# Seven half-size products in place of eight for 19 of 22 unit pairs of a feed-forward's first layer

## The chip, the cores and the metric

One core of one Trainium2 chip runs the whole program. The metric is the device time of one execution in microseconds (us), the median of several runs. The engines are TensorE (PE, matmuls, with PEld for its weight loads), VectorE (DVE), ScalarE (ACT), GpSimd (POOL, here only an issuer of DMA transfers) and SyncE (SP, the main issuer of transfers).

## What is computed

A two-layer encoder is applied to two sequences with shared weights. Each has 16 learned tokens and 256 tokens of 1024 features. A layer adds a mixer (retention and attention, gated) and then a feed-forward to h:

```python
def _swiglu(h, w_ffn_in, w_ffn_out):
    a, u = jnp.split(h @ w_ffn_in, 2, axis=-1)
    return (jax.nn.silu(a) * u) @ w_ffn_out

    for l in range(DEPTH):          # DEPTH = 2
        h = h + _mixer(_rms(h, norm_mix[l]), w_in[l], ...)
        h = h + _swiglu(_rms(h, norm_ffn[l]), w_ffn_in[l], w_ffn_out[l])
    return _rms(h, norm_final)[:, N_META:]
```

D_MODEL is 1024 and D_FF is 2816, so w_ffn_in has 2 x 2816 columns: 22 blocks of 128 for a and 22 for u. All data are 32-bit floats.

## The kernel before

**Tiles.** Activations lie with features on the 128 partitions: eight tiles of 128 features by tokens (272 in layer 0; 256 in the last layer, whose learned tokens are not needed there). Weights are cut into units, one for each block of 128 output columns: eight 128x128 tiles, 512 KB. A unit of the first feed-forward layer is called ("fa", f) for the gate half and ("fu", f) for the other half, f from 0 to 21; the output layer's are "fo0" to "fo2" for three groups of f (8, 7 and 7).

**Precision.** Each operand is split into a high part, rounded to the matmul's format by a ScalarE copy, and a low part, the VectorE subtraction that is left. A product is three matmuls for each feature tile: high by high, high by low, low by high (lines 222 to 224). A unit is thus 24 matmuls for one moving block. In layer 0 the moving block is one sequence (272 columns), and every unit runs twice. In layer 1 most units run once over both sequences (512 columns); where a stage starts they run for each sequence (256 columns). `split` (line 226) makes the parts of activations, `prefetch` (lines 203 to 216) those of weights: per half unit a 256 KB transfer on SP's queue into `wst` (three buffers), `A.copy` to `wh`, and a subtraction to `wl` (four buffers each), two units ahead.

**Norm.** The feed-forward's norm scales a token by r. The kernel before multiplies h by the gain and splits it at once, in `fin_wo` at the end of each unit of the mixer's last layer ("wo"), by `u_split`; r (`norm_scale`, a matmul of ones by the summed squares, two transposes and some ten small VectorE operations) comes later, and the products are scaled after the matmul (`fin_fa`, `fin_fu`).

**Order.** The program is a list of units written out in order (`prog`); steps that belong between units are put off by a number of units (`later`, `due`). A scheduler turns that into one instruction order for each engine at build time. It may place an instruction ahead of earlier ones that it reckons are not ready. At run time each engine goes through its own list in order and waits on semaphores. PSUM has eight banks: three "lin", three "att" and two for the scores of attention ("sc").

For each f before: fa's matmuls, VectorE scales the result, ScalarE tanh, two VectorE operations, fu's matmuls, one VectorE operation and the split into the group's tiles `oh`, `ol` (or `gh`, `gl`; the groups alternate). When a group's f are done its "fo" units run, which add to h.

Of the kernel before, what the change touches and what calls it, by code (L numbers as in the profile page):

```python
# [20 lines left out]
ALU = mybir.AluOpType  # L22
# [65 lines left out]
def hybrid_kernel(tc, ctx, a, y_dram):  # L88
# [13 lines left out]
    def f32(t):  # L102
        return t.bitcast(F32)
# [97 lines left out]
    wq, wready = [], {}  # L201

    def prefetch(n):
        while len(wready) < min(n, len(wq)):
            key = wq[len(wready)]
            ap, kt = unit_ap(key)
            wh = wts.tile([P, KT, P], F32R, tag="wh", name="wh", bufs=NW)
            wl = wts.tile([P, KT, P], F32R, tag="wl", name="wl", bufs=NW)
            for k in range(0, kt, NK):
                n = min(NK, kt - k)  # L210
                st = wts.tile([P, NK, P], F32, tag="st", name="wst", bufs=NST)
                nc.sync.dma_start(st[:, :n], ap[:, k:k + n])
                A.copy(wh[:, k:k + n], st[:, :n])  # L213
                V.tensor_tensor(wl[:, k:k + n], st[:, :n], f32(wh)[:, k:k + n], ALU.subtract)  # L214
            wready[key] = (wh, wl, kt)
# [106 lines left out]
    def later(d, f, *args):  # L322
        steps.append((slot[0] + d, f, args))
# [24 lines left out]
    def layer(l):  # L348
# [376 lines left out]

        def open_group(gi):
            n = GROUPS[gi][1] - GROUPS[gi][0]
            pool, tg = ((act, "o"), (E["wk"], "g"))[gi % 2]
            E["g", gi] = grid(tg + "h", F32R, pool=pool, n=n), grid(tg + "l", F32R, pool=pool, n=n)

        def fin_fa(ps, s, f):
            st["fa", s, f] = t = scratch("fa", s, q0)
            V.tensor_tensor(t, of(ps, s, q0), scale(s, q0), ALU.mult)  # L733

        def fin_fu(pu, s, f):
            gi = next(i for i, (f0, f1) in enumerate(GROUPS) if f0 <= f < f1)
            i = f - GROUPS[gi][0]
            ta, t = st.pop(("fa", s, f)), scratch("ft", s, q0)
            tanh(t, ta)
            V.scalar_tensor_tensor(t, t, 1.0, ta, ALU.add, ALU.mult)  # L740
            V.tensor_tensor(t, t, scale(s, q0), ALU.mult)
# [199 lines left out]
    for key, f, rest in prog:  # L941
        if key is None:
            f(*rest)
        else:
# [6 lines left out]
            due(slot[0])  # L951
# [40 lines left out]
```

## Time and profile before

| | us |
|---|---|
| median of 3 runs (1847.3 to 1849.12) | 1849.12 |
| the profiled execution | 1849.4 |
| its span, first to last instruction | 1847.6 |
| TensorE busy in the span | 1830.0 |
| VectorE busy | 1141.9 |
| ScalarE busy | 796.9 |

The span is what the trace shows; the 1.8 us beside it lie before the first and after the last instruction. Busy time counts an instruction from its start to its end; matmuls are pipelined, so that the durations of neighbours overlap, and what one costs is read from the distance of the starts. The same holds in a smaller measure for VectorE.

### The profile page before, as it was taken

Reading aid. Unit: us, or ns where it says so; the run is one execution under the profiler, and the core shown is the slowest. Engines: PE = TensorE matmul, PEld = TensorE weight load, DVE = VectorE, ACT = ScalarE, POOL = GpSimd, SP = SyncE. Lnnn points to the kernel's source line nnn. Section 1 sums busy time; section 2 is a strip of 40 time slices with the busy share of each in tenths; the row PEclk is TensorE's granted clock in tenths of the full one; section 3 lists DMA queues with packets and bytes.
Section 4 is the critical chain, followed back from the end, with each engine's and each line's share of the span. In section 5 each row is a group of like instructions: output and inputs, shape, how many; then the busy total and the mean of one; then the engine's idle time right before and its main releaser. Section 6 shows DMA issues by size and latency. Waiting matters only on the chain.

```text
span 1847.6 us, 32203 instructions
## 1 busy us (share of the span) xinstructions
PE 1830.0 (99%) x12546; PEld 1701.7 (92%) x12546; DVE 1141.9 (62%) x2789; ACT 796.9 (43%) x1791; POOL 9.9 (1%) x31
## 2 busy tenths in 40 slices
PE   9999999999999999999999999999999999999997
PEld 8999999999999999999998888988888988988887
DVE  7777777776466535545577677676754654444545
ACT  7767753443343313323346566444433433222323
POOL 0000000000000000000000000000000000000000
PEclk9999999999999999999999999999999999999999
DMA  4222212224222323232233222222233232332332
GB/s 152 92 70 64 74 60 69 81 70 133 88 81 92 92 69 104 82 101 86 83 124 98 75 74 64 69 69 81 80 126 94 90 103 91 94 99 82 104 95 70
DMA packets 89624, 162.75 MB, mean 88 GB/s; under 512 B 9728, under 2 KB 18176, under 8 KB 89472
## 3 DMA queue, kind: packets, MB, share of 16 engines
q1 hardware_dynamic: 86608, 153.20, 26.6%
q0 software_dynamic: 1632, 6.42, 1.0%
q8 instruction: 98, 1.61, 0.4%
q10 hardware_dynamic: 1232, 1.08, 0.2%
q14 instruction: 54, 0.44, 0.1%
HBM read 156.47 MB, written 4.19 MB: 87 GB/s over the span
## 4 chain that ended last, share of the span: by engine, by line
PE 94%; DVE 2%; ACT 2%; DMA 1%; issue 1%; SPq 0%; DVEq 0%; ACTq 0%
PE fo L223 5%; PE fu L223 5%; PE fa L224 5%; PE fa L223 5%; PE fu L224 5%; PE fu L222 5%; PE fa L222 5%; PE fo L222 5%; PE fo L224 5%; PE rv L223 2%; PE rv L222 2%; PE rv L224 2%; PE wo L222 2%; PE wo L224 2%; PE ao L222 2%; PE ao L224 2%
## 5 line engine op out<-in xcount | busy, mean ns | idle before, releaser
L213 ACT CAST wh<-wst 128x512 fp32r<-128x512 f32 x576 | 339.9, 613 | 645.6 <-issue 182.1
L214 DVE TENSOR_TENSOR wl<-wst,wh 128x512 fp32r<-128x512 f32 x576 | 381.7, 680 | 130.2 <-ACT wh L213 115.3
L222 PE MATMUL fu<-xh,wh 128*128 128x272 f32 (+2 forms) x544 | 173.8, 319 | 0.0
L224 PE MATMUL fa<-xh,wl 128*128 128x272 f32 (+2 forms) x544 | 173.5, 319 | 0.0
L224 PE MATMUL fu<-xh,wl 128*128 128x272 f32 (+2 forms) x544 | 173.5, 319 | 0.0
L223 PE MATMUL fu<-xl,wh 128*128 128x272 f32 (+2 forms) x544 | 173.4, 319 | 0.0
L222 PE MATMUL fa<-xh,wh 128*128 128x272 f32 (+2 forms) x544 | 173.3, 319 | 0.0
L223 PE MATMUL fa<-xl,wh 128*128 128x272 f32 (+2 forms) x544 | 173.3, 319 | 0.0
L222 PE MATMUL fo<-oh,wh 128*128 128x272 f32 (+2 forms) x420 | 126.5, 301 | 0.0
L223 PE MATMUL fo<-ol,wh 128*128 128x272 f32 (+2 forms) x420 | 126.2, 301 | 0.0
L224 PE MATMUL fo<-oh,wl 128*128 128x272 f32 (+2 forms) x420 | 126.2, 300 | 0.0
L748 DVE SCALAR_TENSOR_TENSOR f<-fo,f 128x272 f32<-128x272 f32 (+2 forms) x84 | 39.6, 471 | 118.5 <-PE fo L224 118.0
L222 PEld LDWEIGHTS fu<-xh,wh 128*128 128x128 f32 x544 | 102.3, 188 | 7.2
L223 PEld LDWEIGHTS fu<-xl,wh 128*128 128x128 f32 x544 | 102.2, 188 | 7.1
L222 PEld LDWEIGHTS fa<-xh,wh 128*128 128x128 f32 x544 | 102.3, 188 | 7.0
L224 PEld LDWEIGHTS fu<-xh,wl 128*128 128x128 f32 x544 | 102.2, 188 | 7.0
L224 PEld LDWEIGHTS fa<-xh,wl 128*128 128x128 f32 x544 | 102.2, 188 | 7.0
L223 PEld LDWEIGHTS fa<-xl,wh 128*128 128x128 f32 x544 | 102.2, 188 | 6.9
L733 DVE TENSOR_TENSOR fa<-fa,rn 128x272 f32<-128x272 f32 (+2 forms) x68 | 35.0, 514 | 110.6 <-PE fa L224 110.5
L742 DVE TENSOR_TENSOR ft<-ft,fu 128x272 f32<-128x272 f32 (+2 forms) x68 | 34.6, 509 | 78.7 <-PE fu L224 78.3
L222 PEld LDWEIGHTS fo<-oh,wh 128*128 128x128 f32 x420 | 79.0, 188 | 2.8
L223 PEld LDWEIGHTS fo<-ol,wh 128*128 128x128 f32 x420 | 78.9, 188 | 2.8
(362 smaller groups left out, 5146.3 us busy)
## 6 DMA issues: line engine op xcount, KB each, us to landing
wst<-in_w_in SPq DMA_DIRECT2D x208, 256.0 KB, 2.7
wst<-in_w_ffn_in SPq DMA_DIRECT2D x176, 256.0 KB, 2.8
wst<-in_w_ffn_out SPq DMA_DIRECT2D x64, 256.0 KB, 2.7
wst<-in_w_att_o SPq DMA_DIRECT2D x32, 256.0 KB, 2.7
wst<-in_w_ret_o SPq DMA_DIRECT2D x32, 256.0 KB, 2.7
wst<-in_w_out SPq DMA_DIRECT2D x32, 256.0 KB, 2.7
wst<-in_w_ffn_out SPq DMA_DIRECT2D x32, 192.0 KB, 2.4
f<-in_x POOLq DMA_DIRECT2D x2, 1088.0 KB, 7.8
```

The source lines that it names most:

```text
L213: A.copy(wh[:, k:k + n], st[:, :n])
L214: V.tensor_tensor(wl[:, k:k + n], st[:, :n], f32(wh)[:, k:k + n], ALU.subtract)
L222: T.matmul(out, wh[:, k], at(hi, s, k, c0), start=(k == 0), stop=False)
L223: T.matmul(out, wh[:, k], at(lo, s, k, c0), start=False, stop=False)
L224: T.matmul(out, wl[:, k], at(hi, s, k, c0), start=False, stop=(k == kt - 1))
L733: V.tensor_tensor(t, of(ps, s, q0), scale(s, q0), ALU.mult)
L742: V.tensor_tensor(t, t, of(pu, s, q0), ALU.mult)
L748: V.scalar_tensor_tensor(hh, of(ps, s, q0), 0.5, hh, ALU.mult, ALU.add)
```

## The change

19 of the 22 pairs (fa, fu) of each layer are no longer computed as four block products by eight feature tiles. The pair is seen as a 2x2 block matrix (fa or fu by lower or upper half of the features) times a 2x2 block matrix (lower or upper features by sequence 0 or 1). Instead of eight half-size block products there are seven (`product`, i = 0 to 6), each of four feature tiles: 12 matmuls over one sequence's columns, in both layers. The first three pairs (NPLAIN) stay as they were.

For the weights four combinations are needed, called a, b, c and d: a is fa itself, d the upper half of fu, c = fu with fu's lower half added onto its upper half and fa's lower half onto its lower half, b from a and c. c is formed by a 512 KB load and two accumulating transfers from POOL's queue. b is formed by VectorE. All four are split. `plan` places these steps at fixed leads ahead of a pair, counted in units (a product counts a quarter).

For the activations three sums and one replaced half are needed (`mix`, with the tiles T), and for those the norm must be applied before the products: `norm_x` replaces `u_split`. The products' results are combined on the way out of PSUM. Products 5 and 6 use the two "sc" banks.

The groups of the output layer no longer alternate between two buffers, the temporary pools of the feed-forward have other sizes, and prefetching goes by position (`prefetch(pos[key])`) with the same two units of lead for plain units.

```diff
-NW, AHEAD, NTMP, NLIN = 4, 2, ((8, 0), (4, 4)), 3
+NW, AHEAD, NTMP, NTMPF, NLIN = 4, 2, ((8, 0), (4, 4)), ((4, 3), (4, 5)), 3
+NPLAIN = 3
...
+    def s_load(key):
+        _, l, f, _ = key
+        fa, fu = a["w_ffn_in"][l, f], a["w_ffn_in"][l, NF + f]
+        c, v, d = s_tmp("wc"), s_tmp("wa"), wts.tile([P, NK, P], F32, tag="st", name="wst", bufs=NST)
+        nc.sync.dma_start(c, fu)
+        nc.gpsimd.dma_start(c[:, NK:], fu[:, :NK], accum_op=ALU.add)
+        nc.gpsimd.dma_start(c[:, :NK], fa[:, :NK], accum_op=ALU.add)
+        nc.sync.dma_start(v, fa)
+        nc.sync.dma_start(d, fu[:, NK:])
+        wready[l, f] = {"c": [c], "a": [v], "d": [d]}
+    def s_tmp(name, tag="q", bufs=3):
+        return E["wk"].tile([P, KT, P], F32, tag=tag, name=name, bufs=bufs)
+    def s_hi(w, nm):
+        pool, tg, n, bufs = {"a": (wts, "w", KT, NW), "b": (wts, "w", KT, NW),
+                             "c": (E["wk"], "c", KT, 1), "d": (E["wk"], "d", NK, 1)}[nm]
+        w[nm] += [pool.tile([P, n, P], F32R, tag=tg + x, name=tg + x, bufs=bufs) for x in "hl"]
+        A.copy(w[nm][1], w[nm][0])
+    def s_lo(w, nm):
+        v, h, t = w[nm]
+        V.tensor_tensor(t, v, f32(h), ALU.subtract)
+        w[nm] = (h, t)
+    def s_1(key):
+        w = wready[key[1:3]]
+        s_hi(w, "a")
+        va, vb, vc = w["a"][0], s_tmp("wb", "wb", 1), w["c"][0]
+        w["b"] = [vb]
+        V.tensor_tensor(vb[:, :NK], va[:, :NK], vc[:, NK:], ALU.add)
+        V.scalar_tensor_tensor(vb[:, NK:], va[:, NK:], -1.0, vb[:, :NK], ALU.mult, ALU.subtract)
+    def s_2(key):
+        w = wready[key[1:3]]
+        s_hi(w, "b")
+        s_lo(w, "a")
...
+    def s_3(key):
+        w = wready[key[1:3]]
+        s_hi(w, "c")
+        s_lo(w, "b")
...
+    def s_4(key):
+        w = wready[key[1:3]]
+        s_hi(w, "d")
+        s_lo(w, "c")
+        s_lo(w, "d")
...
+                if key[3] == 0:
+                    lead = (2.5, 1, 0.75, 0.5, 0.25) if last[0] == "sp" else (3, 2, 2, 1, 1)
+                    jobs.extend((at_ - d, fn, key) for d, fn in zip(lead, (s_load, s_1, s_2, s_3, s_4)))
+                at_ += 0.25
...
         def fin_wo(ps, s, j):
...
-            u_split(s, j, DEPTH + l, q0)
             norm_add(s, hh, q0, j)
             if j == KT - 1:
                 later(LN, norm_scale, s, acc.pop(s), q0)
+                for k in range(0, KT, 2):
+                    later(LN + 1 + k // 4, norm_x, s, k)
+                if s:
+                    for i in range(3):
+                        later(LN + 4 + i, mix, i)
...
         def open_group(gi):
             n = GROUPS[gi][1] - GROUPS[gi][0]
-            pool, tg = ((act, "o"), (E["wk"], "g"))[gi % 2]
-            E["g", gi] = grid(tg + "h", F32R, pool=pool, n=n), grid(tg + "l", F32R, pool=pool, n=n)
+            E["g", gi] = grid("oh", F32R, n=n), grid("ol", F32R, n=n)
...
+        def norm_x(s, k):
+            if s and k % NK == 0:
+                E["xn", k // NK] = E["wk"].tile([P, NK, N - q0], F32, tag="q", name="xn", bufs=3)
+            for i in (k, k + 1):
+                t = E["xn", k // NK][:, i % NK] if s else tmpt("xn")[:, q0:]
+                V.scalar_tensor_tensor(t, E["h"][s][:, i, q0:], gains[:, DEPTH + l, i:i + 1],
+                                       E["r"][s][:, q0:], ALU.mult, ALU.mult)
+                if s == 0:
+                    split(E["uh"][0][:, i, q0:], E["ul"][0][:, i, q0:], t)
+            if s:
+                t = E["xn", k // NK][:, k % NK:k % NK + 2]
+                split(E["uh"][1][:, k:k + 2, q0:], E["ul"][1][:, k:k + 2, q0:], t)
+        def mix(i):
+            b12, b22 = E["xn", 0], E["xn", 1]
+            h0, l0 = f32(E["uh"][0]), f32(E["ul"][0])
+            if i == 0:
+                st["T1"] = t = E["wk"].tile([P, NK, N - q0], F32, tag="wb", name="t1", bufs=1)
+                V.tensor_tensor(t, b12, h0[:, :NK, q0:], ALU.subtract)
+                V.tensor_tensor(t, t, l0[:, :NK, q0:], ALU.subtract)
+                V.tensor_tensor(b12, b12, b22, ALU.subtract)
+                V.tensor_tensor(b22, b22, t, ALU.subtract)
+                split(*E["T"][0], b12)
+            elif i == 1:
+                split(*E["T"][1], b22)
+            elif i == 2:
+                V.tensor_tensor(b22, h0[:, NK:, q0:], b22, ALU.subtract)
+                V.tensor_tensor(b22, b22, l0[:, NK:, q0:], ALU.add)
+                split(*E["T"][2], b22)
+            else:
+                split(E["uh"][1][:, :NK, q0:], E["ul"][1][:, :NK, q0:], st.pop("T1"))
...
+        def product(f, i):
...
+            nm, half, (xh, xl) = (("a", 0, X(0, 0)), ("b", 0, E["T"][1]), ("c", 1, X(1, 0)), ("c", 0, E["T"][0]),
+                                  ("a", 1, X(0, 1)), ("b", 1, X(1, 1)), ("d", 0, E["T"][2]))[i]
+            ps = (att if i % 2 else lin)("sp")[:, :N - q0] if i < 5 else st["p34"][:, i - 5]
+            wh, wl = w[nm]
+            for k in range(NK):
+                o = half * NK + k
+                T.matmul(ps, wh[:, o], xh[:, k], start=k == 0, stop=False)
+                T.matmul(ps, wh[:, o], xl[:, k], start=False, stop=False)
+                T.matmul(ps, wl[:, o], xh[:, k], start=False, stop=k == NK - 1)
+            if i == 0:
...
+                A.copy(st["tu"][:, 0], ps)
...
+            if i == 1:
+                V.tensor_tensor(u2, ps, t1, ALU.subtract)
...
+            elif i == 3:
...
+                V.tensor_tensor(v, ps, u2, ALU.add)
+                V.tensor_tensor(y, p5, u2, ALU.add)
+                V.scalar_tensor_tensor(st["c"][:, 3], v, -1.0, p5, ALU.mult, ALU.subtract)
+            elif i == 4:
+                V.tensor_tensor(st["c"][:, 0], ps, t1, ALU.add)
...
+                tanh(st["v"][:, 0], st["c"][:, 0])
+            elif i == 6:
...
+                V.tensor_tensor(c[:, 1:3], st["p34"], st["yw"], ALU.add)
+                A.activation(v[:, 1], c[:, 1], AF.Tanh, scale=-0.5)
+                V.scalar_tensor_tensor(v, v, 1.0, c[:, :2], ALU.add, ALU.mult)
+                V.tensor_tensor(v, v, c[:, 2:], ALU.mult)
+                s_out(BOTH if q0 else 3, f, v)
...
             for f in fs[n:]:
+                for i in range(7):
+                    L(("sp", l, f, i), None, (product, f, i))
```

## Rows read from the trace of the kernel before

**Rows 1.** The page: TensorE's line of the engine table and the granted clock by slices.

```profile
PE 1830.0 (99%) x12546; PEld 1701.7 (92%) x12546; DVE 1141.9 (62%) x2789; ACT 796.9 (43%) x1791; POOL 9.9 (1%) x31
...
PEclk9999999999999999999999999999999999999999
```

**Rows 2.** The page: the chain that ended last, share of the span by engine.

```profile
PE 94%; DVE 2%; ACT 2%; DMA 1%; issue 1%; SPq 0%; DVEq 0%; ACTq 0%
```

**Rows 3.** Busy time by windows: fa and fu of group 0, each layer.

```profile
core 0: us, PE busy (x) PEld busy (x) DVE busy (x) ACT busy (x) POOL busy (x), PEclk, DMA share, GB/s
554.60:651.80 97.20, 97.20 (x773) 97.12 (x771) 57.71 (x127) 31.58 (x65) 0.00 (x0) 1.00 0.30 88
1468.60:1561.00 92.40, 92.40 (x498) 79.11 (x497) 52.24 (x99) 30.02 (x56) 0.00 (x0) 1.00 0.32 98
```

**Rows 4.** Timeline of TensorE, layer 0: start, duration; the second is 24 matmuls on.

```profile
600.41 0.29 PE L222 MATMUL fu<-xh,wh 128*128 128x272 f32 x1
...
603.45 0.29 PE L222 MATMUL fa<-xh,wh 128*128 128x272 f32 x1
```

**Rows 5.** Timeline of TensorE, layer 1, both sequences; the second is 24 matmuls on.

```profile
1502.46 0.39 PE L222 MATMUL fa<-xh,wh 128*128 128x512 f32 x1
...
1508.02 0.39 PE L222 MATMUL fu<-xh,wh 128*128 128x512 f32 x1
```

**Rows 6.** Timeline of TensorE, layer 1, one sequence; the second is 45 matmuls on.

```profile
1454.15 0.28 PE L222 MATMUL wo<-mh,wh 128*128 128x256 f32 x1
...
1459.45 0.28 PE L222 MATMUL wo<-mh,wh 128*128 128x256 f32 x1
```

**Rows 7.** Timeline of VectorE, layer 0: start, busy us; idle before, releaser.

```profile
601.18 1.29 DVE L214 TENSOR_TENSOR wl<-wst,wh 128x512 fp32r<-128x512 f32 x2
602.40 0.44 DVE L740 SCALAR_TENSOR_TENSOR ft<-ft,fa 128x272 f32<-128x272 f32 x1
...
604.83 0.44 DVE L228 TENSOR_TENSOR ol<-ft,oh 128x272 fp32r<-128x272 f32 x1
605.18 0.69 DVE L214 TENSOR_TENSOR wl<-wst,wh 128x512 fp32r<-128x512 f32 x1
...
607.65 0.44 DVE L740 SCALAR_TENSOR_TENSOR ft<-ft,fa 128x272 f32<-128x272 f32 x1 [0.56 <-ACT ft L231]
...
610.58 0.44 DVE L228 TENSOR_TENSOR ol<-ft,oh 128x272 fp32r<-128x272 f32 x1 [0.48 <-ACT oh L227]
```

**Rows 8.** Groups of VectorE instructions by form: count, busy us, mean ns, idle before.

```profile
L214 DVE TENSOR_TENSOR wl<-wst,wh 128x512 fp32r<-128x512 f32 x544 | 366.1, 687 | 128.8 <-ACT wh L213 113.9 <-PE sc L457 1.1
...
L741 DVE TENSOR_TENSOR ft<-ft,rn 128x272 f32<-128x272 f32 x44 | 19.4, 442 | 1.4
...
L315 DVE SCALAR_TENSOR_TENSOR xn<-f,cst,rn 128x272 f32<-128x272 f32 x24 | 11.3, 496 | 0.0
...
L748 DVE SCALAR_TENSOR_TENSOR f<-fo,f 128x256 f32<-128x256 f32 x24 | 10.1, 422 | 25.7 <-PE fo L224 25.5
...
L228 DVE TENSOR_TENSOR ol<-f,oh 128x544 fp32r<-128x544 f32 x8 | 5.3, 722 | 0.0
```

**Rows 9.** Groups of ScalarE instructions by form.

```profile
L213 ACT CAST wh<-wst 128x512 fp32r<-128x512 f32 x544 | 325.9, 619 | 643.3 <-issue 182.1 <-PE fo L223 116.1 <-PE fa L223 62.9
...
L231 ACT ACTIVATE ft<-fa 128x272 f32<-128x272 f32 x44 | 18.9, 429 | 41.7 <-DVE fa L733 41.7
...
L227 ACT CAST oh<-f 128x544 fp32r<-128x544 f32 x8 | 4.8, 646 | 6.5 <-DVE f L673 6.5
```

**Rows 10.** Timeline of VectorE, layer 1: last steps of the two sequences' r.

```profile
1466.56 0.43 DVE L272 STREAM_TRANSPOSE rn<-rr 128x256 f32<-128x256 f32 x1
...
1475.12 0.45 DVE L272 STREAM_TRANSPOSE rn<-rr 128x256 f32<-128x256 f32 x1
```

**Rows 11.** The page: DMA issues, KB each, median us to landing.

```profile
wst<-in_w_ffn_in SPq DMA_DIRECT2D x176, 256.0 KB, 2.8
...
f<-in_x POOLq DMA_DIRECT2D x2, 1088.0 KB, 7.8
...
f<-in_x SPq DMA_DIRECT2D x2, 544.0 KB, 6.4
```

More of the change, by code (lines that the diff above doesn't have):

```diff
@@ L199, in unit_ap @@
         return a["w_in"][l, W_IN[kind] + j], KT
[L201 to L215, printed above, removed]
+    jobs, wready = [], {}
@@ new lines, in load @@
+    def load(key):
+        ap, kt = unit_ap(key)
+        wh = wts.tile([P, KT, P], F32R, tag="wh", name="wh", bufs=NW)
+        wl = wts.tile([P, KT, P], F32R, tag="wl", name="wl", bufs=NW)
+        for k in range(0, kt, NK):
+            n = min(NK, kt - k)
+            st = wts.tile([P, NK, P], F32, tag="st", name="wst", bufs=NST)
+            nc.sync.dma_start(st[:, :n], ap[:, k:k + n])
+            A.copy(wh[:, k:k + n], st[:, :n])
+            V.tensor_tensor(wl[:, k:k + n], st[:, :n], f32(wh)[:, k:k + n], ALU.subtract)
+        wready[key] = (wh, wl, kt)
@@ new lines, in s_4, with plan @@
+    def s_4(key):
[3 more added lines that the diff above has]
+        s_lo(w, "d")
+    pos = {}
+    def plan():
+        at_, last = 0.0, None
+        for op in prog:
+            key = op[0]
+            if key is None or key in pos:
+                continue
+            pos[key] = at_
+            if key[0] != "sp":
+                jobs.append((at_ - AHEAD, load, key))
+                at_ += 1
+            else:
[3 more added lines that the diff above has]
+                at_ += 0.25
+            last = key
+        jobs.sort(key=lambda j: j[0])
@@ L731, in fin_fa, with s_out @@
+        def s_out(s, f, t):
+            gi = next(i for i, (f0, f1) in enumerate(GROUPS) if f0 <= f < f1)
+            gh, gl = E["g", gi]
+            c0 = q0 if s < 2 else 0
+            split(gh[s][:, f - GROUPS[gi][0], ..., c0:], gl[s][:, f - GROUPS[gi][0], ..., c0:], t)
         def fin_fa(ps, s, f):
             st["fa", s, f] = t = scratch("fa", s, q0)
-            V.tensor_tensor(t, of(ps, s, q0), scale(s, q0), ALU.mult)
+            tanh(t, of(ps, s, q0))
+            V.scalar_tensor_tensor(t, t, 1.0, of(ps, s, q0), ALU.add, ALU.mult)
@@ L735, in fin_fu @@
         def fin_fu(pu, s, f):
[L736 to L741, printed above, removed]
+            t = st.pop(("fa", s, f))
             V.tensor_tensor(t, t, of(pu, s, q0), ALU.mult)
-            gh, gl = E["g", gi]
-            split(at(gh, s, i, q0), at(gl, s, i, q0), t)
+            s_out(s, f, t)
@@ L897, in layer @@
         for gi, (f0, f1) in enumerate(GROUPS):
-            do(open_group, gi)
+            if gi:
+                do(open_group, gi)
             fs = list(range(f0, f1))
-            blocks = [(fs[:2], range(2))] + [([f], pair) for f in fs[2:]] if gi == 0 else [([f], pair) for f in fs]
+            n = NPLAIN if gi == 0 else 0
+            blocks = [(fs[:2], range(2))] + [([f], pair) for f in fs[2:n]] if n else []
             for b, ss in blocks:
@@ L924, in hybrid_kernel @@
     do(lambda: (E["c1"].close(), E["ct"].close()))
-    for op in prog:
-        if op[0] is not None and op[0] not in wq:
-            wq.append(op[0])
+    plan()
     ps = att("warm")
@@ L950, in hybrid_kernel @@
             post(ps, *args)
-            due(slot[0])
+        due(slot[0])
     due(1 << 30)
```

51 lines of the change are left out of this document (42 added, 9 removed).

## Prediction

> **What bounds the kernel now.** First the page's engine table and its slices, to see which engine has no slack: TensorE is busy 99% of the span at a granted clock of full speed in every slice [rows 1]. A busy share is no proof, so next the chain that ended last: 94% of it is TensorE [rows 2]. Then the windows of the two first-layer stretches that the change touches: layer 0 holds TensorE 97.20 of 97.20 us, VectorE 57.71, ScalarE 31.58, DMA share 0.30; layer 1 holds 92.40 of 92.40, VectorE 52.24 [rows 3]. So in these stretches a removed matmul is worth its pitch, and the question is what the other engines do when their load rises. A matmul's duration overlaps the next one's, so I take pitches from starts: 24 matmuls of 272 columns in 3.04 us, 0.1267 us each [rows 4]; 24 of 512 in 5.56 us, 0.2317 [rows 5]; 45 of 256 in 5.30 us, 0.1178 [rows 6].
>
> **Removed: matmuls.** A pair is fa and fu of one f. Before, layer 0 issues 2 units x 2 sequences x 24 = 96 matmuls of 272 columns, 96 x 0.1267 = 12.16 us; layer 1 issues 48 of 512 columns, 48 x 0.2317 = 11.12 us. After, both issue 7 products x 4 feature tiles x 3 = 84: layer 0 of 272 columns, 10.64 us; layer 1 of 256 columns, 9.90 us. The saving is 1.52 and 1.22 us a pair; with 19 pairs a layer 28.9 + 23.2 = 52.1 us. That is all the change can give. Layer 1 saves less because it gives up its 512-column form.
>
> The Trainium skill (TensorE: Matmul & The Clock Gate, Back-to-back issue gap) speaks against that split: it gives a sustained 81 ns per matmul at N=128 and 131 ns at N=512. By a line through these two, an estimate from that page, 84 matmuls of 256 columns would take 8.2 us and 48 of 512 columns 6.3 us, so layer 1 would lose some 36 us. Here 512 columns take 231.7 ns, 1.97 times the 256-column pitch [rows 5, 6]; the trace does not agree, and the measurement decides.
>
> **Added: VectorE, and it is nearly TensorE's load.** Per pair, VectorE forms vb (two 128x512 operations), subtracts the high parts of a, b and c (three of 1024 elements) and of d (one of 512); it unloads the products with five operations one sequence wide and four two sequences wide. By occupation (start to start) 512 elements cost 1.22/2 = 0.61 us and 272 cost 0.35 [rows 7]; that is 1.08 ns an element, so 256 cost 0.33, 544 0.64 and 1024 1.16. Weights: 3 x 0.61 + 3 x 1.16 = 5.3 us. Unloading: layer 0 5 x 0.35 + 4 x 0.64 = 4.3, layer 1 5 x 0.33 + 4 x 0.61 = 4.1. Sum 9.6 us against TensorE's 10.64 in layer 0, 9.4 against 9.90 in layer 1: 90% and 95%. The lower bound of the cost is nothing (VectorE fits under TensorE). The upper takes full durations, 0.687 for 512, 0.722 for 544, 0.442 for 272, 0.422 for 256 [rows 8], and 1.22 for 1024 by their slope: layer 0 10.9, layer 1 10.6; and adds the two places where a pair's chain crosses to ScalarE and back (tanh, then the high copy). Unfilled they idle VectorE 0.56 and 0.48 us [rows 7], with the wider copy about 1.15 together: 12.0 and 11.7 us. The same rows show the first kind filled, two weight halves at 601.18 between fa and ft, so the instruction order does put weight work into such holes. I take values near the lower end: TensorE waits 0.15 us a pair in layer 0 and 0.4 in layer 1, where only 0.5 us is spare: 2.9 + 7.6 = 10.5 us.
>
> ScalarE copies a, b, c (1024 elements) and d, and per pair has three one-sequence operations and one wide copy: by 0.619 for 512, 0.646 for 544 and 0.429 for 272 [rows 9], 3 x 1.03 + 0.62 + 3 x 0.43 + 0.65 = 5.7 us of 10. TensorE's products hide it; uncovered it would cost that.
>
> **Moved: the norm.** Before, the unnormalised u is split inside wo's units and the scale r is applied after the matmul. Now uh needs r first. r of sequence 0 is ready at 1467.0 [rows 10], 1.6 us before layer 1's stretch begins [rows 3], and then eight tiles each need a scaled multiply (0.496 us [rows 8]), a ScalarE copy and a 0.35 subtraction, some 0.85 us of VectorE a tile, beside wo's last residuals and the weights of fa and fu. TensorE eats a tile in 3 x 0.1178 = 0.35 us, or in 0.7 if fa and fu take turns. Sequence 1's r comes at 1475.6 [rows 10], some 4 us before its first unit is due four units after wo; its tiles and the mixes (about 12 us of VectorE for ten operations of 1024 or 1088 elements) stand before the first product. Queued behind them on VectorE are the plain pairs' unloadings and the first pair's weights, and for those TensorE waits. VectorE's work from wo to the first product is about 40 us (two norms 13, mixes 12, six plain units' weights 7, their unloading 5, first pair's weights 5) against some 34 to 36 us of TensorE. Nothing if reordering covers it, 10 a layer if not; I take 5, so 10 us. The removed u_split (0.5 us of VectorE per wo unit) helps a little and is not counted.
>
> **Group ends.** The last pair's chain from product 7 to the low part is 0.72 + 0.43 + 0.72 + 0.72 + 0.65 + 0.72 and four hops of about 0.1 (a tanh wait of 0.56 [rows 7] less its 0.43), 4.3 us; the output unit that follows needs that tile after 21 or 18 matmuls, 2.7 or 2.3 us in layer 0, 4.2 us with 512 columns in layer 1. Unless other units fill in, 1.6 + 2.0 + 2.0 = 5.6 us. The second pair of each group has its loads issued only when the first pair's products start; I put 0.5 us on each of six. Together 8 us (0 to 12). All groups now share one buffer, but its first new write comes a whole pair after the last read, so that costs nothing; without the cover it would be one pair, 10 us, per group.
>
> **Transfers.** A pair moves 1.75 MB in place of 1 MB: two 512 KB and one 256 KB load on SP's queue, two 256 KB accumulating transfers on POOL's queue, which first wait for c's load; POOL is otherwise idle, so nothing is behind them but the next pair's. At share 0.30 before [rows 3], 0.30 x 1.75 x 12.16/10.64 gives 0.60, with room. No row shows an accumulate. From below it costs as a plain 256 KB load, 2.8 us; from above as POOL's 1088 KB, 7.8 us [rows 11]. Load of c (between 2.8 and the 544 KB row's 6.4, say 3.6) plus one accumulate that vb needs: 6.4 to 11.4 us, and if two run one after the other at the upper price 19 to 22. The load is issued ten products (14 to 15 us) ahead and b is needed one product in, with 3.6 us of vb, copy and subtraction before: 12 to 13 us are there. I take nothing, keeping the upper end as a rival.
>
> The Trainium skill (DMA: Bandwidth & Descriptors, Anatomy of one DMA) fits 2.0 us plus bytes/436e3, which makes a 256 KB transfer 2.6 us and 1088 KB 4.6; the POOL row above says 7.8, so the page would make the accumulate cheaper than the trace suggests, and with it the term stays nothing.
>
> **Sum.** -52.1 + 10.5 + 10 + 8 = -23.6 us. The profiled execution took 1849.4 us (span 1847.6 and 1.8 around it), 0.3 above the median of 1849.12. 1849.4 - 23.6 = 1826 us.
>
> **Rivals.** (1) All cover holds: only a few us of the 28.5 are lost, 1797 to 1811. For it: VectorE's bare sum is under TensorE's in both layers, and the order already fills holes. Against: 95% use of an in-order queue. Chance 0.22. (2) VectorE becomes the bound, the one that ends on the other side: at 12.0 and 11.7 us a pair layer 0 saves 0.16 x 19 = 3 and layer 1 loses 0.6 x 19 = 11, and with the 18 us of moved work it comes to 1875. It decides from a mean of 11.17 us a pair: 19 x (12.16 + 11.12 - 2 x 11.17) = 18. For it: no slack in layer 1 and four crossings to ScalarE on each pair. Against: the holes at 601.18 are filled. Chance 0.22, a third of it mild, 1840 to 1846. (3) The accumulating transfers are late: at 22 us c and a each hold one of three slots for about 25 us, two slots a pair, 16.7 us a pair, 19 x (16.7 - 10.8 + 16.7 - 10.3) = 234 us more, 2060; at 13 to 14 us only some us. Chance 0.07. (4) In this stage a 256-column matmul costs more than half of a 512-column one, as when weight loads no longer hide: at the next wider pitch, 0.1267, layer 1's 84 take 10.64 us, 14 us less is saved, 1840. The 256-column rows speak against it. Chance 0.04. It is the mechanism of the TensorE page of the Trainium skill named above. The forecast keeps 0.45, its own range 1812 to 1840.
>
> Faster by over 0.2% (3.7 us, about what a measurement here can tell from no change): 0.45 + 0.22 + 0.07 + 0.04 = 0.78; within 0.2% 0.04; slower 0.18. The range runs from 1799, near the full saving, to 1856, into rival (2); about 0.18 lies outside.
>
> **What would show it.** Right: some 84 matmuls a pair at 0.127 and 0.118 us; pair to pair 10.6 to 11 us in layer 0 and 10 to 10.7 in layer 1; VectorE over 90% busy there; TensorE gaps of some us after wo and at group ends; granted clock still full. Wrong if VectorE is 98% busy with pairs above 11.2 us, or if vb waits for POOL's transfer, or if TensorE has no gaps at all.

## The result and the profile after

The changed kernel takes 1893.33 us (median; 1890.15 to 1896.92), the kernel before 1848.8 us beside it: ratio 1.0247, interval 1.0234 to 1.026. It is 2.5% slower, where 1826 was forecast. The profiled execution has a span of 1890.3 us against 1847.6.

The page after, in its engine table, the clock by slices, the chain by engine and the DMA issues (KB each, median us to landing):

```profile
PE 1812.6 (96%) x13002; PEld 1712.7 (91%) x13002; DVE 1293.2 (68%) x2948; ACT 862.6 (46%) x1833; POOL 76.5 (4%) x107
...
PEclk9999999999999999899999999999999999999999
...
PE 69%; DVE 12%; DMA 11%; ACT 4%; issue 4%; DVEq 0%; POOL 0%; ACTq 0%; POOLq 0%
...
wc<-in_w_ffn_in SPq DMA_DIRECT2D x38, 512.0 KB, 3.6
wc<-in_w_ffn_in POOLq DMA_DIRECT2D x76, 256.0 KB, 5.8
wa<-in_w_ffn_in SPq DMA_DIRECT2D x38, 512.0 KB, 4.6
```

TensorE is busy for only 17 us less than in [rows 1], and the span grew by 43: it now stands idle for 78 us, not 18. The chain of [rows 2] was 94% TensorE; now VectorE and DMA hold 23% of it. VectorE, the engine that I had feared for, is busy for only 68% of the span.

Cut at the first matmul of each stretch, in both traces, the first layer (ff) and the output layer (fo) of the six groups take, in us:

| | 0: ff, fo | ff, fo | ff, fo | 1: ff, fo | ff, fo | ff, fo |
|---|---|---|---|---|---|---|
| before | 97.2, 48.4 | 84.6, 42.3 | 84.6, 42.7 | 89.3, 44.4 | 77.8, 38.9 | 77.8, 39.3 |
| after | 94.8, 54.8 | 84.2, 52.2 | 82.9, 46.9 | 93.0, 53.1 | 81.6, 47.5 | 81.1, 40.1 |

Summed: the first layer 517.6 against 511.3, the output layer, whose matmuls the diff does not touch, 294.6 against 256.0. So the first layer shows nothing of the 52 us saved, and nearly the whole net loss appears where no matmul was changed. (The second window of [rows 3] runs 2.9 us into the output layer; cut here, that stretch is 89.3.) Windows after, layer 0 (group 0's ff, group 1's ff and fo, and the stretch in which TensorE restarts in that fo) and layer 1 (group 1's ff and fo):

```profile
core 0: us, PE busy (x) PEld busy (x) DVE busy (x) ACT busy (x) POOL busy (x), PEclk, DMA share, GB/s
552.80:647.60 94.80, 91.71 (x713) 89.95 (x712) 84.01 (x148) 44.45 (x74) 12.26 (x14) 1.00 0.57 151
702.40:786.60 84.20, 78.47 (x590) 77.29 (x590) 61.28 (x97) 34.64 (x54) 10.50 (x12) 0.96 0.59 139
786.60:838.80 52.20, 45.20 (x339) 44.98 (x338) 24.07 (x41) 10.93 (x18) 1.43 (x2) 0.90 0.32 94
...
792.90:803.10 10.20, 5.86 (x26) 5.86 (x27) 4.86 (x8) 1.69 (x4) 0.00 (x0) 0.50 0.27 72
...
1628.60:1710.20 81.60, 74.53 (x590) 73.01 (x590) 59.70 (x98) 33.77 (x54) 10.48 (x12) 0.96 0.59 142
1710.20:1757.70 47.50, 41.12 (x255) 36.33 (x254) 21.73 (x36) 10.71 (x18) 0.64 (x2) 0.93 0.35 106
```

The reader is to see three things. In a group of seven pairs VectorE is busy for 61.28 of 84.20 us, 73%, so it does not set the pace. DMA is at 0.59, where I had put 0.60. And the granted clock is below one: at 792.90 it is 0.50, the lower of the two levels (1.2 GHz), for 10.2 us around a stop of TensorE. That output layer is explained to the tenth: 42.3 before, 7.0 us of standing still, and half of the 5.86 busy us at half clock make 52.2. The mean clock of the whole run is 0.982, against 0.998 before: some 68 us at the lower level ((1 - 0.982) x 1890.3 / 0.5) in place of some 8.

Who waited, by engine and releaser (us in total, times, longest):

```profile
DVE wb L250 <- DMA wc<-in_w_ffn_in: 57.4, 19, 4.0
...
ACT wh L214 <- DMA wst<-in_w_ffn_out: 33.2, 18, 5.4
...
PE fo L299 <- ACT oh L304: 25.6, 5, 7.0
PE sp L867 <- DVE c L884: 19.0, 11, 3.5
...
SPq L224 <- DVE cl L242: 59.6, 11, 9.7
```

The first line is the sign that the prediction gave for its own failure: vb (tile `wb`) waits for POOL's transfer. The last is the other half: SP's load of the next c waits for VectorE, for `cl`, the low part of an earlier c. Timelines of VectorE, SP and POOL in group 1 of layer 0 (start, duration, idle before):

```profile
747.23 0.69 DVE L250 TENSOR_TENSOR wb<-wa,wc 128x512 f32<-128x512 f32 x1 [2.78 <-DMA wc<-in_w_ffn_in]
...
750.24 1.22 DVE L242 TENSOR_TENSOR cl<-wc,ch 128x1024 fp32r<-128x1024 f32 x1
...
751.49 0.33 SPq L224 DMA_DIRECT2D wc<-in_w_ffn_in  x1
...
755.53 0.88 POOL L225 DMA_DIRECT2D wc<-in_w_ffn_in  x1 [11.61 <-DVE dl L242]
...
761.41 0.69 DVE L250 TENSOR_TENSOR wb<-wa,wc 128x512 f32<-128x512 f32 x1 [3.44 <-DMA wc<-in_w_ffn_in]
762.02 0.43 DVE L883 TENSOR_TENSOR yw<-sp,tu 128x272 f32<-128x272 f32 x1
...
763.96 1.22 DVE L242 TENSOR_TENSOR cl<-wc,ch 128x1024 fp32r<-128x1024 f32 x1
...
765.20 0.33 SPq L224 DMA_DIRECT2D wc<-in_w_ffn_in  x1
```

Read it as a ring. SP issues the load of c at 751.49, at the end of a `cl`, which was the last reader of one of the three raw buffers. It lands after 3.5 us, and 4.0 us after the load POOL issues the accumulating transfer (the label there names VectorE's `dl`, which ended 0.2 us after the landing); 5.9 us later that has landed and VectorE, idle for 3.44 us, starts `wb`. Only behind that, and behind the unloadings that had piled up, comes `cl` of the pair before (2.55 us on), takes 1.22 and frees the buffer for the next load, at 765.20. One turn: 4.04 + 5.88 + 2.55 + 1.22 + 0.02 = 13.7 us a pair, against 10.6 us of matmuls. SP's loads of c in this group start at 710.87, 724.14, 738.06, 751.49, 765.20 and 779.12, 13.7 us apart in the mean. TensorE starts the group's first four pairs 10.6 us apart, because the order makes a pair's parts ahead of its products, and falls behind after that. The instruction that frees the buffer stands on VectorE behind the instruction that waits for the transfer into the next one.

At the end of the group the lag arrives at TensorE. Timelines of SP, ScalarE and TensorE there:

```profile
784.65 1.15 SPq L213 DMA_DIRECT2D wst<-in_w_ffn_out  x2
788.41 0.33 SPq L227 DMA_DIRECT2D wa<-in_w_ffn_in  x1
...
791.77 0.51 ACT L214 CAST wh<-wst 128x384 fp32r<-128x384 f32 x1 [5.35 <-DMA wst<-in_w_ffn_out]
792.18 0.42 ACT L308 ACTIVATE v<-c 128x272 f32<-128x272 f32 x1
...
796.54 0.65 ACT L304 CAST oh<-v 128x544 fp32r<-128x544 f32 x1 [1.20 <-DVE v L894]
...
797.24 0.59 PE L299 MATMUL fo<-oh,wh 128*128 128x272 f32 x1 [7.00 <-ACT oh L304]
```

ScalarE waits 5.35 us for output weights. SP holds further ones behind a load of a that waits for its buffer until 788.41, but those that ScalarE waits for were issued at 784.65, ahead of that. They were slow to land, beside the accumulating transfers that POOL issued at 783.12 and 783.66 (DMA issue at 784.65):

```profile
wst<-in_w_ffn_out SPq DMA_DIRECT2D x1, 192.0 KB, 7.1
```

Output weights issued from 783 to 796 took at most 7.1 us; in the like stretch of the kernel before (781 to 794) 2.7, and of run 4 below, which has no accumulating transfer (766 to 779), 4.4. Behind ScalarE's wait stands the last pair's tanh (792.18); the pair's high copy ends at 797.2, and TensorE had run dry 7 us before.

### The profile page after: what moved, and what is told of

It is laid out like the page before. It is cut to its first block, busy times and chain, and to the rows that moved or that the text cites. A ratio compares the mean times of both kernels' runs of the same rounds, so it can differ in the third digit from the quotient of the medians.

```text
span 1890.3 us, 33475 instructions
## 1 busy us (share of the span) xinstructions
PE 1812.6 (96%) x13002; PEld 1712.7 (91%) x13002; DVE 1293.2 (68%) x2948; ACT 862.6 (46%) x1833; POOL 76.5 (4%) x107
## 3 DMA queue, kind: packets, MB, share of 16 engines
q10 hardware_dynamic: 1232, 1.08, 0.2%
## 4 chain that ended last, share of the span: by engine, by line
PE 69%; DVE 12%; DMA 11%; ACT 4%; issue 4%; DVEq 0%; POOL 0%; ACTq 0%; POOLq 0%
DMA wc<-in_w_ffn_in 6%; PE fo L299 4%; PE fo L300 4%; PE fo L301 4%; DMA wst<-in_w_ffn_out 2%; DMA wa<-in_w_ffn_in 2%; PE rv L300 2%; PE rv L299 2%; PE rv L301 2%; PE ao L300 2%; PE ao L301 2%; PE ao L299 2%; PE aq L299 2%; PE gr L301 2%; PE gr L300 2%
## 5 line engine op out<-in xcount | busy, mean ns | idle before, releaser
L214 ACT CAST wh<-wst 128x512 fp32r<-128x512 f32 (+1 forms) x424 | 250.9, 610 | 367.6 <-PE fo L300 73.9
L215 DVE TENSOR_TENSOR wl<-wst,wh 128x512 fp32r<-128x512 f32 (+1 forms) x424 | 281.7, 677 | 126.6 <-ACT wh L214 120.5
L299 PE MATMUL fo<-oh,wh 128*128 128x272 f32 (+2 forms) x616 | 190.5, 310 | 25.6 <-ACT oh L304 25.6
L301 PEld LDWEIGHTS fo<-oh,wl 128*128 128x128 f32 x616 | 119.7, 194 | 4.1
L869 PE MATMUL sp<-xh,wl 128*128 128x272 f32 (+1 forms) x304 | 87.3, 287 | 2.3 <-DVE wl L242 2.3
L867 PE MATMUL sp<-xh,wh 128*128 128x272 f32 (+1 forms) x304 | 87.4, 287 | 0.0
L868 PE MATMUL sp<-xl,wh 128*128 128x272 f32 (+1 forms) x304 | 86.9, 286 | 0.0
L250 DVE TENSOR_TENSOR wb<-wa,wc 128x512 f32<-128x512 f32 x38 | 26.3, 692 | 75.3 <-DMA wc<-in_w_ffn_in 57.4
L299 PE MATMUL wo<-mh,wh 128*128 128x272 f32 (+2 forms) x224 | 67.8, 303 | 0.0
L300 PE MATMUL wo<-ml,wh 128*128 128x272 f32 (+2 forms) x224 | 67.4, 301 | 0.0
L301 PE MATMUL wo<-mh,wl 128*128 128x272 f32 (+2 forms) x224 | 67.4, 301 | 0.0
L238 ACT CAST wh<-wb 128x1024 fp32r<-128x1024 f32 x38 | 39.6, 1043 | 42.3 <-DVE wb L251 28.8
## 6 DMA issues: line engine op xcount, KB each, us to landing
wst<-in_w_in SPq DMA_DIRECT2D x208, 256.0 KB, 2.7
wc<-in_w_ffn_in POOLq DMA_DIRECT2D x76, 256.0 KB, 5.8
wst<-in_w_ffn_out SPq DMA_DIRECT2D x64, 256.0 KB, 3.0
wst<-in_w_ffn_in SPq DMA_DIRECT2D x62, 256.0 KB, 3.0
wst<-in_w_att_o SPq DMA_DIRECT2D x32, 256.0 KB, 2.8
wst<-in_w_ret_o SPq DMA_DIRECT2D x32, 256.0 KB, 2.8
```

Of the source, the lines that this page charges most:

```text
L238: A.copy(w[nm][1], w[nm][0])
L250: V.tensor_tensor(vb[:, :NK], va[:, :NK], vc[:, NK:], ALU.add)
L867: T.matmul(ps, wh[:, o], xh[:, k], start=k == 0, stop=False)
L868: T.matmul(ps, wh[:, o], xl[:, k], start=False, stop=False)
L869: T.matmul(ps, wl[:, o], xh[:, k], start=False, stop=k == NK - 1)
```

## The experiments

Each was timed in the same job as the kernel before (1847.4 to 1848.2 us there). Stretches are cut as in the table above.

**1. no_accumulate.** Lines 225 and 226 go, so that c is the plain weights of fu and the result is another:

```diff
-        nc.gpsimd.dma_start(c[:, NK:], fu[:, :NK], accum_op=ALU.add)
-        nc.gpsimd.dma_start(c[:, :NK], fa[:, :NK], accum_op=ALU.add)
```

> Leaves out the two accumulating transfers, so c is the plain second half of the weights. Theory A (the raw buffers are a loop: c's 3.6 us load, its 5.4 us accumulate, then 4.3 us of VectorE until the previous pair's c is released, 13.5 us a pair): without the accumulate the loop is about 8 us, below TensorE's 10.6 and 9.9, so the groups of seven pairs fall from 84 and 81 us to 74 to 78 and 69 to 74, and the kernel to 1835 to 1855. Theory B (VectorE's added work and its crossings to ScalarE set the pace): VectorE's work is untouched, the groups stay at 81 to 84 and the time at 1880 to 1893.

1808.98 us, ratio 0.9793 (0.9778 to 0.9809), faster than either theory had. Groups 1 and 2 take 74.0 in layer 0 and 69.4 in layer 1 for seven pairs, 10.57 and 9.91 us a pair, with TensorE free of gaps (window of layer 0's group 1):

```profile
694.30:768.30 74.00, 74.00 (x591) 74.00 (x590) 65.40 (x103) 37.59 (x57) 0.00 (x0) 1.00 0.40 122
```

84 matmuls at 0.1267 and 0.1178 us are 10.64 and 9.90: in these groups the saving was there in full, and the two transfers cost the kernel 84 us.

**2. raw_loads_on_POOL.** Was it SP's queue, where the output weights stand behind loads that wait for a buffer?

```diff
-        nc.sync.dma_start(c, fu)
+        nc.gpsimd.dma_start(c, fu)
...
-        nc.sync.dma_start(v, fa)
+        nc.gpsimd.dma_start(v, fa)
```

> The raw loads of a and c are issued from POOL's queue and no longer from SP's. Theory A2 (the 39 us that the output sections lose come from a raw load of the next group that waits in SP's queue for a buffer, with the output layer's weights behind it): the six output sections fall from 54.8, 52.2, 46.9, 53.1, 47.5 and 40.0 us to 42 to 48 and 39 to 44, the pairs stay, the kernel comes to 1855 to 1870. Theory B2 (the last pair's results are late because VectorE is behind): the output sections stay as they are, 1885 to 1895.

1908.95 us, 1.0332 (1.0317 to 1.0348). The output layers stay at 58.7, 50.2, 47.6 and 56.0, 47.3, 41.4. Freeing SP's queue does not bring them back: ScalarE still waits for output weights, 37.4 us in all against 33.2. The kernel is 16 us slower still, over both expectations. That the loads now stand behind the transfers on POOL may be why; it was not taken apart.

**3. all_plain.** The old products for all 22 pairs, without the mixes, but the norm moved ahead of the matmuls as in the change:

```diff
-            n = NPLAIN if gi == 0 else 0
-            blocks = [(fs[:2], range(2))] + [([f], pair) for f in fs[2:n]] if n else []
+            n = len(fs)
+            blocks = [(fs[:2], range(2))] + [([f], pair) for f in fs[2:n]] if gi == 0 else [([f], pair) for f in fs]
...
-            if n:
-                do(mix, 3)
```

> No pair uses the seven products; the norm before the products, the new pools and the one group buffer stay. If the moved norm costs what the prediction put, 5 us a layer, the kernel takes 1855 to 1862. If reordering hides it, 1849 to 1852. If it were a main cause of the loss it would be over 1865.

1852.08 us, 1.0024 (1.0013 to 1.0034). Only group 0's first layer differs from before: 99.4 and 92.2 against 97.2 and 89.3. The moved norm by itself costs some 4 to 5 us; the mixes, which the prediction counted in its 10, are not in this run.

**4. sums_on_VectorE.** The two sums by two 128x512 adds of VectorE, behind the plain loads:

```diff
-        nc.gpsimd.dma_start(c[:, NK:], fu[:, :NK], accum_op=ALU.add)
-        nc.gpsimd.dma_start(c[:, :NK], fa[:, :NK], accum_op=ALU.add)
         nc.sync.dma_start(v, fa)
+        V.tensor_tensor(c[:, NK:], c[:, NK:], c[:, :NK], ALU.add)
+        V.tensor_tensor(c[:, :NK], c[:, :NK], v[:, :NK], ALU.add)
```

> c is formed by two more 128x512 VectorE additions a pair in place of the two accumulating transfers; the result is the same. Theory A: the transfer chain shrinks by 5 us a pair for 1.2 us of VectorE, which is busy 73% of the groups now, so the groups fall to 76 to 80 and 71 to 76 us, the kernel to 1845 to 1865. Theory B: 1.2 us more on the engine that sets the pace, 38 pairs, 46 us slower than the changed kernel, 1930 to 1940.

1811.97 us, 0.98 (0.9784 to 0.9817): VectorE gets 1.2 us a pair more and the kernel is 81 us faster than the change, below both expectations. Group 1 of both layers:

```profile
695.60:769.60 74.00, 74.00 (x590) 74.00 (x589) 70.09 (x114) 37.58 (x57) 0.00 (x0) 1.00 0.38 119
1579.80:1649.20 69.40, 69.40 (x591) 69.40 (x590) 65.73 (x110) 34.60 (x54) 0.00 (x0) 1.00 0.40 125
```

VectorE is 95% busy and TensorE waits for nothing. That VectorE sets the pace is refuted.

**5. four_raw_buffers.** The accumulating transfers stay; a fourth raw buffer, paid for with smaller temporaries:

```diff
-NTMPF = ((4, 3), (4, 5))
+NTMPF = ((3, 3), (4, 4))
...
-    def s_tmp(name, tag="q", bufs=3):
+    def s_tmp(name, tag="q", bufs=4):
```

> Four raw buffers for a and c in place of three (paid for by one small temporary fewer in each layer); the accumulating transfers stay. Theory A (a loop through the buffers: c's load 3.6 us, first accumulate 5.4, then VectorE until the previous c's low part has released its buffer): the load of the next c no longer waits for that release, the wait of VectorE for the accumulate goes from about 3 us a pair to under 1, the groups fall to 74 to 78 and 69 to 74 us, the kernel to 1810 to 1840. Theory C (the accumulate's traffic itself slows the other transfers and engines, whatever the buffers): 1870 to 1895.

1817.23 us, 0.9834 (0.9816 to 0.9851). Page (DMA issue) and window of layer 0's group 1:

```profile
wc<-in_w_ffn_in POOLq DMA_DIRECT2D x76, 256.0 KB, 5.4
...
694.60:768.70 74.10, 74.10 (x590) 74.10 (x589) 65.81 (x103) 37.86 (x57) 10.51 (x12) 1.00 0.67 163
```

The same bytes and nearly the same latency, with the highest DMA share so far, 0.67, and no gap. So in the groups of seven it is neither the traffic nor what the transfers do to other engines. With a buffer more a load is let go earlier: five loads of c in this group were issued 13.3 to 14.0 us ahead of their `wb`, in the change 9.0 to 10.1. The output layers keep a part of the loss (50.0, 42.6, 43.8 and 46.5, 44.6, 39.9).

**6. plain_copies_on_POOL.** The same two transfers without the addition (c holds other values then): `accum_op=ALU.add` is dropped from both.

> The two transfers on POOL's queue stay in place, size and order but copy and no longer add, so c's contents are others. Theory A with the accumulate's own slowness: a plain 256 KB transfer from POOL lands in 3.5 to 4.5 us in place of 5.8, the loop shrinks by 1 to 2 us a pair, 30 to 60 us are won back, 1830 to 1865. If any second transfer behind the first is as bad as an accumulating one: 5.5 us again and 1885 to 1895.

1846.93 us, 0.9997 (0.9988 to 1.0007). DMA issue and wait:

```profile
wc<-in_w_ffn_in POOLq DMA_DIRECT2D x76, 256.0 KB, 3.6
...
DVE wb L250 <- DMA wc<-in_w_ffn_in: 37.0, 18, 3.3
```

The addition makes 2.2 us of the 5.8, and those 2.2 us are worth 46 us of the kernel. By the ring, 13.7 - 2.2 = 11.5 us a turn, still above 10.6; accordingly groups 1 and 2 lie between the change and run 1, with 78.2 and 77.1 in layer 0, 77.1 and 74.0 in layer 1.

**7. b_behind_c_low.** Three buffers and the accumulating transfers as in the change; only the order on VectorE: `wb` of a pair is put behind `cl` of the pair before.

```diff
-        V.tensor_tensor(t, v, f32(h), ALU.subtract)
+        lo = V.tensor_tensor(t, v, f32(h), ALU.subtract)
+        if nm == "c":
+            E["cl"] = lo.ins
...
-        V.tensor_tensor(vb[:, :NK], va[:, :NK], vc[:, NK:], ALU.add)
+        with tc.issue_after(E["cl"]) if "cl" in E else ExitStack():
+            V.tensor_tensor(vb[:, :NK], va[:, :NK], vc[:, NK:], ALU.add)
```

> Only VectorE's order is changed: the sum that makes b, which waits for the accumulate, is queued behind the previous pair's subtraction that makes c's low part and frees c's raw buffer. Theory D (the fixed order is what closes the loop: the buffer's release stands behind an instruction that waits for the transfer of the next c): the loop opens with three buffers and the accumulates kept, 1815 to 1850. Theory A in its plain form (three buffers are too few for a 9 to 10 us transfer chain): the loop stays, at most 1 us a pair is won, 1855 to 1893.

1832.47 us, 0.9916 (0.9899 to 0.9932), 61 us faster than the change with the same instructions. Page, wait and window (layer 0's group 1):

```profile
wc<-in_w_ffn_in POOLq DMA_DIRECT2D x76, 256.0 KB, 6.0
...
DVE wb L253 <- DMA wc<-in_w_ffn_in: 2.9, 1, 2.9
...
704.60:778.60 74.00, 74.00 (x591) 74.00 (x590) 65.48 (x102) 36.32 (x57) 10.50 (x12) 1.00 0.71 171
```

The transfers are as slow as ever and no longer late: the wait of 57.4 us is down to 2.9. One turn from the timelines of VectorE and SP:

```profile
743.50 1.23 DVE L242 TENSOR_TENSOR cl<-wc,ch 128x1024 fp32r<-128x1024 f32 x1
744.76 0.33 SPq L224 DMA_DIRECT2D wc<-in_w_ffn_in  x1
745.00 0.68 DVE L253 TENSOR_TENSOR wb<-wa,wc 128x512 f32<-128x512 f32 x1
```

`cl` frees the buffer before `wb`, and SP's loads of c are 10.6 us apart (713.06, 723.63, 734.20, 744.76) and no longer 13.7. This is the run that shows the ring, since nothing but the order was changed. The first group of each layer is not cured: 96.5, 55.1 and 91.6, 55.0.

**8. b_behind_c_low_loads_on_POOL.** Is that rest SP's queue? Runs 7 and 2 together.

> The order of b_behind_c_low, and the 512 KB loads of c and a issued from POOL instead of SP, so that the loads of the output weights on SP's queue never stand behind a load that waits for a buffer. Theory E (in b_behind_c_low the output layer of each layer's first group kept 55.1 and 55.0 us because SP held its output weights behind c's load, issued at 642.10 when c's low part ended at 642.08): that output layer falls to 49 to 51 us in layer 0 and 45 to 48 in layer 1, the total to 1815 to 1823. Rival F (the last pair of the first group is late by itself, its chain of unloading, tanh and low part being behind on VectorE and ScalarE): it stays at 53 to 56 us, total 1830 to 1836. If the loads on POOL come later than on SP because they now stand behind the accumulating transfers, the groups behind the first rise above 74.0 and 69.4 us.

1845.99 us, 0.9992 (0.9983 to 1.0002). The first groups take 99.1, 58.6 and 96.8, 54.0, the others 74.0 and 69.4 as in run 7. The total lies above both expectations, and the first layer of the first groups has grown too. Theory E falls: with the loads of a and c off SP's queue, TensorE still waits for the last pair's high copy (timelines of VectorE, ScalarE and TensorE, layer 0):

```profile
655.00 0.43 DVE L889 TENSOR_TENSOR c<-sp,tu 128x272 f32<-128x272 f32 x1
...
657.86 0.62 ACT L214 CAST wh<-wst 128x512 fp32r<-128x512 f32 x1 [3.85 <-DMA wst<-in_w_ffn_out]
658.39 0.42 ACT L311 ACTIVATE v<-c 128x272 f32<-128x272 f32 x1
...
664.35 0.60 PE L302 MATMUL fo<-oh,wh 128*128 128x272 f32 x1 [7.32 <-ACT oh L307]
```

The tanh's input is ready at 655.43. But ScalarE's order has the copy of an output weight first, idles 3.85 us for it, and the tanh starts at 658.39. That weight was issued at 652.23 and took 5.6 us to land. So the last pair's chain is late, as the rival said, and a part of its delay is a wait that stands ahead of it on ScalarE. No run moved that copy behind the tanh. Four buffers or sums on VectorE cure most of the loss (fo 50.0 and 49.2 in layer 0), the order alone does not.

**9. sums_on_POOL.** The sums of run 4 by GpSimd (`G.tensor_tensor` in place of `V.tensor_tensor`).

> c is formed by two 128x512 additions on GpSimd in place of the two accumulating transfers; the result is the same. VectorE's load is that of the changed kernel. If GpSimd takes up to 2 us for one, the chain is 3.6 + 2 to 4 us, shorter than with the accumulate: 1800 to 1820, level with or a little below the sums on VectorE. If it takes 4 us or more, or holds VectorE up, 1820 to 1880.

1861.52 us, 1.0068 (1.0053 to 1.0083). Groups by form, GpSimd's two adds and VectorE's `wb`:

```profile
L227 POOL TENSOR_TENSOR wc<-wc,wa 128x512 f32<-128x512 f32 x38 | 64.0, 1685 | 156.6 <-DMA wa<-in_w_ffn_in 156.5
L226 POOL TENSOR_TENSOR wc<-wc 128x512 f32<-128x512 f32 x38 | 56.6, 1490 | 547.5 <-DMA wc<-in_w_ffn_in 442.8 <-DVE f L915 40.3 <-DVE c L891 30.3
...
L250 DVE TENSOR_TENSOR wb<-wa,wc 128x512 f32<-128x512 f32 x38 | 40.9, 1076 | 9.5 <-DMA wa<-in_w_ffn_in 7.5 <-POOL wc L226 0.9 <-issue 0.7
```

A sum takes less time than a transfer (1.5 to 1.7 us against 5.8), within the 2 us for which I had expected 1800 to 1820 (1820 to 1880 if it held VectorE up). Yet VectorE pays: `wb` takes 1.08 us in place of 0.69, and group 1 takes 75.3 and 74.8. How much of the 50 us over run 4 is this slowing, and how much the longer way over GpSimd, was not taken apart. The Trainium skill (SBUF — State Buffer, Who interferes with whom) says that a VectorE instruction with two SBUF inputs contends with a GpSimd instruction that reads SBUF. This trace agrees: the 28 `wb` that overlap a GpSimd add take 1.22 us in the mean, the other ten 0.68.

**10. sums_on_VectorE_4_buffers.** Runs 4 and 5 together.

> The sums on VectorE and four raw buffers together. With the sums on VectorE the groups of seven already run at TensorE's pace (74.0 and 69.4 us), so a fourth buffer can only take what the ends of groups and the first group still lose, some 10 us in all: 1803 to 1812. If it is level with three buffers, the buffer count mattered only through the accumulate's latency.

1808.05 us, 0.9786 (0.9772 to 0.9801), the lowest median of all, 2.1% faster than before; over run 4 the gain lies within the runs' spread (1807.65 to 1810.7 and 1808.72 to 1812.4).

**11. sums_on_VectorE_2_plain.** Run 4 with `NPLAIN = 2`, one product pair more in each layer.

> The sums on VectorE and 20 of 22 pairs by seven products. TensorE saves 1.5 + 1.2 us more, 1809; if the mixes, which then have a pair's time less before the first product, are late, 1812 to 1825.

1829.16 us, 0.99 (0.9886 to 0.9915). Group 0's first layer grows from 92.3 and 90.6 to 102.9 and 98.4, the rest is unchanged. The normalised and mixed inputs are late when a plain pair less covers them, by more than I had put (1812 to 1825); in layer 0 TensorE waits 1.23 us at 598.27 for the low part of a T tile.

**12. one_more_VectorE_step.** Run 4 with `cl` computed twice, 1.2 us a pair more.

> The sums on VectorE, and each pair repeats one VectorE subtraction of 1024 elements (1.14 us of occupation, same result). VectorE is 95% busy in the groups of seven now. Theory: from about 100% of TensorE's 10.6 and 9.9 us VectorE sets the pace; 10.0 + 1.1 in layer 0 and 9.4 + 1.1 in layer 1 are over it by 0.5 to 0.6 us a pair, so the groups go to 77 to 82 and 73 to 78 us and the kernel to 1830 to 1860. If VectorE had room left, 1812 to 1818.

1824.64 us, 0.9873 (0.9857 to 0.989): 13 us over run 4, for some 43 us of VectorE (38 x 1.13). Layer 1's group 1:

```profile
1589.30:1662.10 72.80, 70.73 (x593) 69.86 (x592) 69.69 (x110) 33.31 (x53) 0.00 (x0) 1.00 0.38 118
```

Here VectorE begins to bind, at 96% of a stretch that is 3.4 us longer; layer 0 has 74.4 and 75.1, still nearly none. Most of the growth lies in the first groups' first layer (98.7 and 95.1 against 92.3 and 90.6). Whether the load or the longer way to `cl` does it was not separated; the time lies between the two expectations.

## Why the prediction was wrong

**Removed matmuls, right.** 10.57 and 9.91 us a pair against my 10.64 and 9.90, where nothing else holds TensorE (runs 1, 4, 5).

**Transfers, the step that failed.** "The load is issued ten products (14 to 15 us) ahead [...] 12 to 13 us are there. I take nothing." The latency was within my bounds: c's load and one accumulate took 4.0 + 5.9 = 9.9 us where I had 6.4 to 11.4. The lead was wrong. The program writes the load down ten products ahead, but SP issues it when one of three buffers is free, and I never asked what frees it. It is `cl` of an earlier pair, which VectorE's order has behind the `wb` that waits for the transfer; so the load has no lead at all, and its latency, the unloadings and `cl` add up to 13.7 us a pair. Runs 5 and 7 open the ring at two different places (a buffer, the order), each with the accumulate as slow as before, and both take the loss away in the groups of seven; run 6 shortens it by 2.2 us a turn. Rival (3) had the right suspects, late transfers and three slots. But it counted a slot's holding time and not what its release stands behind, and so put the price "at 13 to 14 us" at "only some us". In the groups of seven, where the ring turns six times between first and last pair, that makes 6 x 3.1 = 19 us in layer 0; group 1 measured 84.2 + 52.2 against run 4's 74.0 + 43.6, 18.8. That this comes so close is in part luck, since the measured loss holds the clock's share and the wait for output weights too. It is no exact rule: in layer 1 it gives 6 x 3.8 = 23 where 19.0 was measured, and both last groups lost less (12.3 in layer 0).

**VectorE, its load right, its effect wrong.** I reckoned 9.6 and 9.4 us a pair. In run 1, which has the change's VectorE work, it is busy for 65.40 / 7 = 9.3 in layer 0 and 63.32 / 7 = 9.0 in layer 1 (1575.1 to 1644.5); in run 4, with the sums, for 10.0 and 9.4. I then put 10.5 us of TensorE waits on it: in the groups of seven of run 4, at 95%, they are nothing. Rival (2), VectorE as the bound, ended on the right side by the wrong mechanism: it was 73% busy in a slower kernel, and more work for it made the kernel faster.

**Moved norm.** 4 to 5 us for the norm alone (run 3). With the mixes, group 0's first layer should fall by five pairs' saving, 97.2 - 7.6 = 89.6 and 89.3 - 6.1 = 83.2; in run 4 it takes 92.3 and 90.6, 10 us more in all, and in run 1 92.0 and 86.2, 5 more. That is within my 0 to 20, and in run 4 my 10.

**Group ends.** Put at 8 us. In the change the output layers lose 38.6; in run 4 they lose 5.9 (261.9 against 256.0). The last pair's own chain is thus about as I had it. The rest is the lag of the ring and ScalarE's wait for late output weights, which I had not thought of, with the clock on top; how they share the loss was not taken apart.

**Rival (4) is refuted** by the 69.4 us of layer 1's groups. With the transfers' cost avoided, run 4 puts the change's own sum at 1812, just over rival (1)'s 1811 and at the lower edge of my own 1812 to 1840.

**Open.** Why the first group of each layer stays slow when only the order is mended is not settled. SP's queue is excluded by run 8. ScalarE's wait for an output weight, ahead of one of the last pair's two tanh steps, is there in run 7 as well (2.59 us at 653.35, 4.28 at 1552.6), but it was not removed by itself. The clock, which I expected to stay full, was not; its share in the loss was taken apart from the stops only in the one output layer above.

## What to carry to other kernels

A load's lead is not where the program writes it but when its buffer is freed: follow each new transfer's buffer back to its last reader, and ask whether that reader stands, on its in-order engine, behind the instruction that waits for this very transfer; if so, the whole latency is paid once a turn, at any share of busy time. A busy share of 95% on the helping engine cost nothing here in the groups of seven, while two transfers a pair on an idle queue cost 84 us: latency in a ring outranks load. Look as well at what stands behind a wait for a transfer on an engine: at the group ends it was the tanh that TensorE needed. Before a sum is moved from an engine to a transfer, compare the two durations (0.61 us of VectorE's time against 5.8 us until landing).

## What was not expected of the hardware

- An accumulating transfer of 256 KB issued from POOL landed in 5.4 to 6.0 us; without the addition, from the same queue, in 3.6. The Trainium skill's fit (DMA: Bandwidth & Descriptors, Anatomy of one DMA) does not speak of an addition; by it 256 KB would take 2.6 us, an estimate that is too low here for both.
- Where accumulating transfers ran, others landed late. Of the 96 transfers of output weights, 22 to 26 took over 4 us in each of the five kernels that have them (the change and runs 2, 5, 7 and 8), the slowest 7.1; in the kernel before and the other runs it was 1 to 9, the slowest 5.2.
- TensorE streamed without a gap beside a VectorE that was 95% busy with in-order work on which each product depends (run 4, 74.00 of 74.00 us).
- Around a stop of TensorE of 7.0 us the granted clock was at its lower level for 10.2 us (from 792.90), so the stop cost more than its length: 7.0 us of standing still became 9.9.
